# Second sets of seven products in three more up pairs of each layer, and the shared keys' row built later, in a two-layer hybrid decoder on one core

## The chip, the core and the metric

The kernel runs on one core of a Trainium2 chip. The metric is the device time of one execution, in microseconds (us). Names used below: PE is TensorE, PEld its weight loads, DVE is VectorE, ACT is ScalarE, POOL is GpSimd, SP is SyncE. A line such as L402 is that line of the kernel before. The change adds lines ahead of it, so the same code stands 5 lines lower in the changed kernel from there on (L402 is L407, L378 is L383, L596 is L601); L229 and L230 stay.

## The reference

Two layers over 256 tokens of width 2048: a chunked gated linear attention (GLA) in layer 0, a forgetting attention (FoX) in layer 1, each beside four heads of attention into 256 memory tokens. FoX's keys and values are projected from the residual after layer 0, once. Each layer ends in a gated feed-forward block with a causal convolution of width 3 between its projections:

```python
def conv_ffn(h, w_up, conv_w, conv_b, w_down):          # h: 256 x 2048
    u = causal_dwconv(h @ w_up, conv_w, conv_b)         # w_up: 2048 x 11264
    a, val = split_cols(u, [FFN_HIDDEN, FFN_HIDDEN])    # 5632 each
    return (jax.nn.silu(a) * val) @ w_down              # w_down: 5632 x 2048
def fox_shared_kv(x, g_kv, w_kv, b_f):
    hs = rmsnorm(x, g_kv)
    k, v, fl = split_cols(hs @ w_kv, [FOX_WIDTH, FOX_WIDTH, FOX_HEADS])
```

All of it is fp32. The outputs are one 256 x 2048 array.

## The kernel before, in words

**Products.** Every fp32 product is made of three matmuls of a rounded type. A weight tile of 128x1024, called raw, is loaded on SP's queue (L224); ACT rounds it to `whi` (L229) and DVE subtracts that from raw to get `wlo` (L230). The activations are kept in two such parts as well, so a product is (x high, w high), (x low, w high) and (x high, w low): two matmuls with `whi` and one with `wlo`. A tile pool holds 4 each of raw, whi and wlo, so ACT's split of a tile waits until PE has read the one four tiles earlier.

**Up pairs.** The up projection of a layer is done in 11 up pairs (0 to 10; up pair j//4 makes the gate and value columns of four hidden chunks j to j+3). An up pair runs over the 16 chunks k of the normed input; a chunk is one unit: one weight tile and 12 matmuls of 128x512 into four banks (two token blocks by two column halves). Matmuls of up and down pairs are issued in L402.

**Sets of seven products.** Two units with neighbouring chunks k and k+1 can be done together by a Strassen-like scheme with seven products instead of eight: 7x3 = 21 matmuls instead of 2x12 = 24. Such a set (`pair_steps`, L381 to L459) needs sums of the activations, prepared once for a chunk pair (`input_sums`, `token_sums`), and sums of the two weight tiles: raw2 tiles of their own, four subtractions of 128x512 on DVE (L427 to L430), and four splits by L377 on ACT and L378 on DVE (one of 512, three of 1024). After the last set of a pair, `early` scales what its products gave into tiles u; the pair's other units go on in the other banks, and `late` adds them up at the end.

Before, every up pair has one set, at k = 6. The first up pair after each of the first two parts of the hidden chunks (`PARTS`), which are up pairs 5 and 8, has a second at k = 11 through `more`, whose sums are computed anew each time into the tile `dsum` 0. The order of a pair's steps is that of k, so the sets stand at places 7 and 8, and 12 and 13. Down passes between the parts (f = 0 and 2, each 16 or 12 units) have sets too. The hidden chunks' pairs are ordered: up 0 to 4, two down passes, up 5 to 7, two down passes, up 8 to 10, then the last passes (the first of them called wide in the code).

**Work beside it.** An up pair's result is turned through DRAM on POOL's queue (`turn`, `far_away`, L640); when it is back, ACT makes the convolution's taps (L1384) and DVE adds and multiplies them (L1391, L1404). `tick` gives these steps out: after each unit the pair gains a credit (`drive`, 1.45 a unit), each step costs 0.5 to 1.0 of it, and a turn's first tap may come 8 ticks after the turn at the earliest.

**The shared keys' row.** FoX's key columns are three panels fk(0), fk(1), fk(2) (L333) of 8 units each, two units to a step for the first two (`two_tm`). The keys are scaled by 1/rms of each token, which must lie along a row: `row` (L585 to L599) builds two diagonal tiles dg on DVE (L594), multiplies them with ones on PE (L596, into the work bank ps_t) and copies the result on ACT (L598). It is called by a hook after unit 2 of fk(1); its first reader is L1160 (`keys`).

**Masks.** One constant tile `mask` of 1120 columns holds the identity, FoX's mask, the scan's mask, the level masks and an eye; it is loaded on SP's queue.

Of the kernel before, what the change touches and what calls it, by code (L numbers as in the profile page):

```python
# [36 lines left out]
SEVEN_MORE = 11  # L37

# [107 lines left out]
def _trunk(ctx: ExitStack, tc: tile.TileContext, xt, xtok, memt, wp, wgu, gns, gfin, cnv, par, msk, out):  # L146
# [13 lines left out]
    mask = const.tile([P, M_N], F32, name="mask")  # L160
# [3 lines left out]
    scanmask = mask[:, M_SCAN : M_SCAN + T]  # L164
# [216 lines left out]
    def pair_steps(units, src, sums, flip, pool, early, late):  # L381
# [360 lines left out]
    with tc.tile_pool(name="load", bufs=1) as lp:  # L742
# [57 lines left out]
        for u in range(8):  # L800
# [3 lines left out]
            elif u == 3:  # L804
                for b in range(2):
                    S.activation(mv[0][:, b, :], mv[0][:, b, :], AF.Copy, scale=nrm.col()[:, b : b + 1])
                with tc.issue_after(loads[-1].ins):
                    for i in range(KC):
                        nc.sync.dma_start(xf[i], xt[i])
                    nc.sync.dma_start(part, par)  # L810
                    nc.sync.dma_start(mask[:, M_FOX:], msk[:, M_FOX:])
# [20 lines left out]
    def gla(nx):  # L832
        h, mix = bufB, bufA
        with tc.tile_pool(name="gla", bufs=1) as gp:
            scratch[0] = gp

# [28 lines left out]
            def gates(hd):  # L865
# [7 lines left out]
                for c in range(2):  # L873
# [11 lines left out]
                    V.tensor_tensor_scan(bc[:, c, :], scanmask, mz, 0.0, ALU.mult, ALU.add)  # L885
# [110 lines left out]
            def core(hd):  # L996
# [36 lines left out]
                eye = mask[:, M_EYE:].bitcast(I32).unsqueeze(1).to_broadcast(ins.shape)  # L1033
                V.copy_predicated(ins, eye, ps[:, 192:320].rearrange("p (b t) -> p b t", b=2))
                for li, B in enumerate(LEVELS):
                    H = B // 4
                    p3 = levels[li].rearrange("p (b c) -> p b c", b=2)
                    m3 = mask[:, M_LVL + NVER * li : M_LVL + NVER * (li + 1)].bitcast(I32)
# [96 lines left out]
    def fox(nx, vt, stash):  # L1135
        hk, hq, mix = bufB, bufA, bufB
        with (
# [228 lines left out]
    def ffn(l, nx, h, m, ys, zs, landing, then, pool, temps, last=None, spare=None):  # L1366
        with tc.tile_pool(name=f"ffn{l}", bufs=1) as fp:
# [46 lines left out]
            def input_sums(k, tag="usum", at=None):  # L1414
# [4 lines left out]
                t = held(tag, k if at is None else at)  # L1419
# [76 lines left out]

            up_sums = {k: input_sums(k) for k in SEVEN_UP}
# [3 lines left out]
            more = {}  # L1501
            for p, (lo, hi) in enumerate(PARTS[:-1]):
                while done < hi + 4:
                    drive(up_pair(done, more))
                    more = {}
# [7 lines left out]
                more = {SEVEN_MORE: input_sums(SEVEN_MORE, "dsum", 0)}  # L1513
            lo, hi = PARTS[-1]
            while done < hi:
                drive(up_pair(done, more))
# [247 lines left out]
```

## Time and profile before

| | |
|---|---|
| time, median of 3 runs (lowest to highest) | 2221.74 us (2221.12 to 2222.1) |
| the profiled execution's own time | 2221.88 us |
| its span, first to last instruction | 2220.1 us |
| its mean granted TensorE clock | 0.999 |
| PE busy | 2207.2 us, 99% of the span |
| DVE busy | 1788.5 us, 81% |
| ACT busy | 1418.8 us, 64% |
| POOL busy | 136.1 us, 6% |
| up and down pairs of L402, layer 0 | 457.6 to 1110.8 us of the span |
| the same of layer 1 | 1500.8 to 2154.8 us |

The profile is one execution; the durations below come from it, and its own time is 0.14 us over the median. What lies between span and time is 1.78 us. A view by windows lists for a stretch of time the busy us of each engine with the count of its instructions (x); matmuls overlap in the records, so PE's own counts can include one that began earlier, while the count of PEld is the number of matmuls started. A group's row gives busy time and mean ns of one instruction, and behind a second bar the idle time of the engine just before them with what ended it. In the view in order of time a row has start, length, engine, line, operation and operands, and in brackets the idle time before it and its releaser.

### The profile page before, as it was taken

To read this page: it belongs to the slowest core of one execution; us is meant where nothing else is said; L and a number is where in the kernel's file an instruction comes from. 1 tells how busy PE (TensorE), PEld (TensorE's weight loads), DVE (VectorE), ACT (ScalarE), POOL (GpSimd) and SP (SyncE) were. 2 spreads that over 40 slices of the span, in tenths; PEclk is the share of its full clock that TensorE was granted. 3 is DMA by queue.
4 is the path that set the end of the run, shared out by engine and by line. 5 is a ranking of instruction groups with operands and counts; after the bars stand their busy time and mean duration, and the time that the engine had idled before them with its cause. 6 is when DMAs were issued, how large, how long until landed. Compare 5 with 4: busy or idle time off the path is not lost.

```text
span 2220.1 us, 30058 instructions
## 1 busy us (share of the span) xinstructions
PE 2207.2 (99%) x10323; PEld 1853.8 (84%) x10323; DVE 1788.5 (81%) x2654; ACT 1418.8 (64%) x2257; POOL 136.1 (6%) x257
## 2 busy tenths in 40 slices
PE   9999999999999999999999999999999999999998
PEld 7888888888888888888887998888888888888886
DVE  7768977688897888888978569668888888888896
ACT  6655664556787468656865455555787647665874
POOL 0000000001100000001110000000101000100100
PEclk9999999999999999999999999999999999999999
DMA  9767667778777567667777767777677757766674
GB/s 356 245 223 222 192 191 242 248 231 253 229 243 258 185 221 244 227 225 240 226 250 244 233 203 244 224 240 244 218 240 246 240 196 239 234 236 222 225 258 150
DMA packets 165633, 515.47 MB, mean 232 GB/s; under 512 B 20700, under 2 KB 41832, under 8 KB 165480
## 3 DMA queue, kind: packets, MB, share of 16 engines
q1 hardware_dynamic: 148488, 461.36, 63.6%
q0 software_dynamic: 16416, 51.40, 7.6%
q8 instruction: 81, 1.33, 0.2%
q10 hardware_dynamic: 576, 0.79, 0.1%
q14 instruction: 72, 0.59, 0.1%
HBM read 469.68 MB, written 43.79 MB: 231 GB/s over the span
## 4 chain that ended last, share of the span: by engine, by line
PE 95%; issue 2%; DVE 1%; DMA 1%; ACT 0%; POOL 0%; DVEq 0%; ACTq 0%; POOLq 0%
PE acc L402 30%; PE acc L333 23%; PE ps_s L402 15%; PE ps_o L402 7%; PE ps_t L402 7%; PE acc L305 3%; PE acc L260 3%; PE acc L363 2%; PE acc L258 1%; PE ps_s L333 1%; DVE wlo L230 0%; PE ps_s L1011 0%; DMA raw<-wp 0%; DMA fvt<-far 0%; PE ps_o L686 0%
## 5 line engine op out<-in xcount | busy, mean ns | idle before, releaser
L230 DVE TENSOR_TENSOR wlo<-raw,whi 128x1024 fp32r<-128x1024 f32 (+4 forms) x739 | 876.8, 1196 | 256.6 <-ACT whi L229 232.6
L229 ACT ACTIVATE whi<-raw 128x1024 fp32r<-128x1024 f32 (+4 forms) x739 | 760.4, 1037 | 447.4 <-PE acc L333 166.3
L333 PE MATMUL acc<-whi,B 128*128 128x512 f32 (+3 forms) x1248 | 292.0, 370 | 0.0
L377 ACT ACTIVATE whi<-raw 128x1024 fp32r<-128x1024 f32 (+1 forms) x136 | 129.8, 954 | 190.7 <-PE acc L402 75.5
L333 PEld LDWEIGHTS acc<-whi,B 128*128 128x128 f32 x1248 | 227.1, 188 | 28.0
L378 DVE TENSOR_TENSOR wlo<-raw,whi 128x1024 fp32r<-128x1024 f32 (+1 forms) x136 | 148.0, 1091 | 63.3 <-ACT whi L377 58.8
L402 PE MATMUL acc<-whi,mix 128*128 128x512 f32 x764 | 194.6, 389 | 0.0
L402 PE MATMUL acc<-whi,B 128*128 128x512 f32 x750 | 193.0, 389 | 0.0
L402 PEld LDWEIGHTS acc<-whi,mix 128*128 128x128 f32 x764 | 143.3, 188 | 30.2 <-ACT whi L229 0.2
L402 PEld LDWEIGHTS acc<-whi,B 128*128 128x128 f32 x750 | 140.8, 188 | 29.6
L333 PE MATMUL acc<-wlo,B 128*128 128x512 f32 (+3 forms) x624 | 158.6, 369 | 0.0
L333 PEld LDWEIGHTS acc<-wlo,B 128*128 128x128 f32 x624 | 114.6, 188 | 14.5
L1384 ACT ACTIVATE tap<-yzu,cw 128x256 f32<-128x256 f32 x264 | 123.5, 531 | 1.5 <-DMA yzu<-far 1.5
L1384 ACT ACTIVATE tap<-fvt,cw 128x256 f32<-128x256 f32 x264 | 123.3, 529 | 0.8 <-DMA fvt<-far 0.8
L1391 DVE TENSOR_TENSOR tap<-tap,tap 128x1024 f32<-128x1024 f32 x88 | 107.3, 1219 | 1.1 <-ACT tap L1384 1.0
L402 PE MATMUL acc<-wlo,mix 128*128 128x512 f32 x382 | 107.5, 389 | 0.0
L402 PE MATMUL acc<-wlo,B 128*128 128x512 f32 x375 | 107.3, 389 | 0.0
L402 PE MATMUL ps_s<-whi,mix 128*128 128x512 f32 x386 | 106.1, 389 | 0.0
L402 PE MATMUL ps_s<-whi,B 128*128 128x512 f32 x342 | 93.5, 389 | 0.0
L402 PEld LDWEIGHTS ps_s<-whi,mix 128*128 128x128 f32 x386 | 72.5, 188 | 15.3
L402 PEld LDWEIGHTS acc<-wlo,mix 128*128 128x128 f32 x382 | 71.7, 188 | 15.0
L402 PEld LDWEIGHTS acc<-wlo,B 128*128 128x128 f32 x375 | 70.4, 188 | 14.7
(498 smaller groups left out, 3802.3 us busy)
## 6 DMA issues: line engine op xcount, KB each, us to landing
raw<-wp SPq DMA_DIRECT2D x743, 512.0 KB, 4.5
fvt<-far POOLq DMA_DIRECT2D x100, 128.0 KB, 5.3
raw<-wp SPq DMA_DIRECT2D x32, 384.0 KB, 3.5
far<-yu POOLq DMA_DIRECT2D x22, 512.0 KB, 5.8
far<-yzu POOLq DMA_DIRECT2D x22, 512.0 KB, 5.4
yzu<-far POOLq DMA_DIRECT2D x88, 128.0 KB, 5.0
raw<-wp SPq DMA_DIRECT2D x24, 388.0 KB, 4.7
x<-xtok SPq DMA_DIRECT2D x8, 512.0 KB, 6.6
```

The costliest lines, as they stand in the source:

```text
L229: casts.append(S.activation(hi[:, s], raw[:, s], AF.Copy))
L230: lows.append(V.tensor_tensor(lo[:, s], raw[:, s], hi[:, s].bitcast(F32), ALU.subtract))
L258: mm = TE.matmul(acc[p][c][:, :T], w[:, s], both[:, 0, :], start=False, stop=end and j == 3)
L260: mm = TE.matmul(acc[p][c], w[:, s], both, start=u == j == 0, stop=end and j == 3)
L305: mm = TE.matmul(acc[b][:, :n], src[kcs[j] - base][:, part, b * P : (b + 1) * P], w, start=u == 0 and low == part == j == 0, stop=u == end ...
L333: mm = TE.matmul(acc[b][:, :n], src[kc - base][:, part, b * P : (b + 1) * P], ready[low][:, j * n : (j + 1) * n], start=i == low == part = ...
L363: mm = TE.matmul(acc[b][:, :n], src[kc - base][:, part, b * P : (b + 1) * P], w, start=i == low == part == j == 0, stop=i == end and low = ...
L377: casts.append(S.activation(hi[:, :n], src, AF.Copy))
L378: lows.append(V.tensor_tensor(lo[:, :n], src, hi[:, :n].bitcast(F32), ALU.subtract))
L402: r = TE.matmul(bank[name], x, w, start=name not in begun, stop=last)
L1384: S.activation(by_run(taps[i][:, s, c, i:]), zs[slot][:, :, 2 * c + s], AF.Copy if i else AF.Identity, bias=0.0 if i else w[3], scale=w[2 ...
L1391: V.tensor_tensor(taps[0], taps[0], taps[n][:, :, :, :T], ALU.add)
```

## The change

Up pairs 1, 5, 6, 8 and 9 (`MORE_IN`) have a second set, at chunks 11 and 12, instead of 5 and 8. In these pairs both sets come two places earlier than by their chunk (`ahead` = 2): at the 5th and the 10th place, with the single units in their own order around them. The sums of chunks 11 and 12 are computed once a layer, within up pair 0 after its unit 13, into a tile of their own that stays. The turns' waits and the credit are altered: 7 ticks instead of 8 for the first turn of a pair that stands ahead of a pair of `MORE_IN`, and 1.7 instead of 1.45 a unit within such a pair. To have room, `mask` keeps 512 columns; the other 608 come in a tile `gmask` of the GLA stage, loaded on POOL's queue. The hook that built the shared keys' row after unit 2 of fk(1) goes; `row` is called after unit 3 of fk(2).

```diff
+MORE_IN = (1, 5, 6, 8, 9)
...
-    mask = const.tile([P, M_N], F32, name="mask")
+    mask = const.tile([P, M_SCAN], F32, name="mask")
...
-    def pair_steps(units, src, sums, flip, pool, early, late):
+    def pair_steps(units, src, sums, flip, pool, early, late, ahead=0):
...
+        single = [k for k in range(n) if k not in sums and k - 1 not in sums]
         plan = []
-        k = 0
-        while k < n:
-            plan.append(k)
-            k += 2 if k in sums else 1
+        at = 0
+        while at < n:
+            if at + ahead in sums:
+                plan.append(at + ahead)
+                at += 2
+            else:
+                plan.append(single.pop(0))
+                at += 1
...
+            gmask = gp.tile([P, M_N - M_SCAN], F32, name="gmask")
+            nc.gpsimd.dma_start(gmask, msk[:, M_SCAN:])
...
-            two_tm([fk(0), fk(1)], 8, 2, {(1, 2): nx.row,
-                                          (1, 3): lambda: nx.land(spare[1]), (1, 5): nx.take})
+            two_tm([fk(0), fk(1)], 8, 2, {(1, 3): lambda: nx.land(spare[1]), (1, 5): nx.take})
             step = fk(2)
             for u in range(8):
                 step(u)
+                if u == 3:
+                    nx.row()
...
-            def up_pair(j, more={}):
+            def up_pair(j):
...
-                turns = [turn(j + 2 * h_, 8) for h_ in range(2)]
+                second = j // 4 in MORE_IN
+                turns = [turn(j + 2 * h_, 7 if not h_ and j // 4 + 1 in MORE_IN else 8) for h_ in range(2)]
...
-                return pair_steps(where["up", l, j], h, {**up_sums, **more}, count[2] % 2, pool, early, late)
+                return pair_steps(where["up", l, j], h, {k: up_sums[k] for k in (*SEVEN_UP, SEVEN_MORE)[: 1 + second]},
+                                  count[2] % 2, pool, early, late, 2 * second)
...
+                if k == 13:
+                    up_sums[SEVEN_MORE] = input_sums(SEVEN_MORE)
...
+            def drive_up(j):
+                drive(up_pair(j), 1.7 if j // 4 in MORE_IN else 1.45)
...
-                more = {SEVEN_MORE: input_sums(SEVEN_MORE, "dsum", 0)}
```

**Place one: PE in up pair 1 of layer 0, behind its fourth unit.** The names B_99 to B_114 are chunks 0 to 15 of the normed input, ps_o, ps_s, ps_t and acc are banks, usum is a tile of sums. Before, the fifth unit follows, chunk 4 (B_103):

```order
L402 MATMUL ps_o<-whi,B_103 128x512 x2
L402 MATMUL ps_s<-whi,B_103 128x512 x4
L402 MATMUL ps_t<-whi,B_103 128x512 x2
L402 MATMUL ps_o<-wlo,B_103 128x512
L402 MATMUL ps_s<-wlo,B_103 128x512 x2
L402 MATMUL ps_t<-wlo,B_103 128x512
L402 MATMUL ps_o<-whi,B_104 128x512 x2
```

In the changed kernel the set of chunks 6 and 7 (B_105, B_106) stands there, and chunk 4 begins behind its first matmuls:

```order
L407 MATMUL acc<-whi,B_105 128x512 x2
L407 MATMUL acc<-wlo,B_105 128x512
L407 MATMUL ps_o<-whi,B_106 128x512 x2
L407 MATMUL ps_s<-whi,usum 128x512
L407 MATMUL ps_o<-wlo,B_106 128x512
L407 MATMUL ps_s<-whi,usum 128x512
L407 MATMUL ps_s<-wlo,usum 128x512
L407 MATMUL acc<-whi,usum 128x512 x6
L407 MATMUL ps_s<-whi,B_106 128x512 x2
L407 MATMUL acc<-wlo,usum 128x512 x2
L407 MATMUL ps_o<-whi,B_103 128x512 x2
```

The set moved up by two places; a second such set, of chunks 11 and 12, follows after chunks 4, 5 and 8, where there were 24 matmuls of single units.

**Place two: PE in the shared keys' panels.** B_111 and B_112 are two chunks of a weight tile of fk(1); dg and onesr are the operands of the row's two products. Before, these lie amid the matmuls with `whi` of one unit:

```order
L333 MATMUL acc<-whi,B_111 128x512 x2
L333 MATMUL acc<-whi,B_112 128x512 x2
L333 MATMUL acc<-whi,B_111 128x512 x2
L596 MATMUL ps_t<-dg,onesr 128x256
L333 MATMUL acc<-whi,B_112 128x512
L596 MATMUL ps_t<-dg,onesr 128x256
L333 MATMUL acc<-whi,B_112 128x512
L333 MATMUL acc<-wlo,B_111 128x512
```

In the changed kernel they stand between the fourth and the fifth unit of fk(2):

```order
L333 MATMUL acc<-wlo,B_105 128x512
L333 MATMUL acc<-wlo,B_106 128x512
L333 MATMUL acc<-wlo,B_105 128x512
L333 MATMUL acc<-wlo,B_106 128x512
L601 MATMUL ps_t<-dg,onesr 128x256 x2
L333 MATMUL acc<-whi,B_107 128x512 x2
L333 MATMUL acc<-whi,B_108 128x512 x2
L333 MATMUL acc<-whi,B_107 128x512 x2
```

Only the two products and ACT's copy of them move; DVE builds the diagonals dg at the same place of its order as before. Over the whole program PE has 18 matmuls of 128x512 fewer.

More of the change, by code (lines that the diff above doesn't have):

```diff
@@ L810, in _trunk @@
                     nc.sync.dma_start(part, par)
[L811 removed]
+                    nc.sync.dma_start(mask[:, M_FOX:], msk[:, M_FOX:M_SCAN])
         with tc.issue_after(nrm.made.ins):
@@ L1500, in ffn @@
             done = 4
-            more = {}
             for p, (lo, hi) in enumerate(PARTS[:-1]):
                 while done < hi + 4:
-                    drive(up_pair(done, more))
-                    more = {}
+                    drive_up(done)
                     done += 4
@@ L1512, in ffn @@
                 sums.clear()
-                more = {SEVEN_MORE: input_sums(SEVEN_MORE, "dsum", 0)}
             lo, hi = PARTS[-1]
             while done < hi:
-                drive(up_pair(done, more))
-                more = {}
+                drive_up(done)
                 done += 4
```

12 lines of the change are left out of this document (6 added, 6 removed).

## The prediction

> **What bounds the kernel now.** I read the page first: its line of busy times, then the chain of work that ended last.
>
> ```profile
> PE 2207.2 (99%) x10323; PEld 1853.8 (84%) x10323; DVE 1788.5 (81%) x2654; ACT 1418.8 (64%) x2257; POOL 136.1 (6%) x257
> ...
> PE 95%; issue 2%; DVE 1%; DMA 1%; ACT 0%; POOL 0%; DVEq 0%; ACTq 0%; POOLq 0%
> PE acc L402 30%; PE acc L333 23%; PE ps_s L402 15%; PE ps_o L402 7%; PE ps_t L402 7%; PE acc L305 3%; PE acc L260 3%; PE acc L363 2%; PE acc L258 1%; PE ps_s L333 1%; DVE wlo L230 0%; PE ps_s L1011 0%; DMA raw<-wp 0%; DMA fvt<-far 0%; PE ps_o L686 0%
> ```
>
> PE is busy for 99% of the span and makes 95% of the chain; L402, which the change touches, is 59% of it. DVE's 81% is an average, so I next read it stage by stage: a window for each pair, cut at the first matmul of the pair and of the next one. In order: up pair 1, up pair 4, down passes f = 0 (without a set) and f = 2 (two sets), up pairs 5 (two sets), 6, 8 (two sets), 9, 10, and the wide pass, all of layer 0.
>
> ```profile
> core 0: us, PE busy (x) PEld busy (x) DVE busy (x) ACT busy (x) POOL busy (x), PEclk, DMA share, GB/s
> 500.58:543.54 42.96, 42.96 (x191) 35.47 (x189) 34.11 (x40) 32.03 (x51) 5.46 (x10) 1.00 0.78 240
> 629.45:672.41 42.96, 42.96 (x190) 35.48 (x189) 39.19 (x51) 33.02 (x54) 5.47 (x10) 1.00 0.78 247
> 672.41:715.94 43.53, 43.53 (x193) 36.04 (x192) 33.71 (x37) 29.74 (x49) 5.46 (x10) 1.00 0.80 271
> 715.94:758.34 42.40, 42.40 (x187) 34.92 (x186) 38.81 (x52) 22.30 (x26) 0.00 (x0) 1.00 0.54 180
> 758.34:800.75 42.41, 42.41 (x187) 34.92 (x186) 33.71 (x38) 22.93 (x25) 0.00 (x0) 1.00 0.57 191
> 800.75:843.72 42.97, 42.97 (x190) 35.48 (x189) 35.19 (x44) 32.60 (x52) 5.50 (x10) 1.00 0.79 247
> 951.41:993.81 42.40, 42.40 (x187) 34.91 (x186) 36.52 (x46) 23.46 (x26) 0.00 (x0) 1.00 0.60 195
> 993.81:1036.78 42.97, 42.97 (x190) 35.48 (x189) 34.16 (x40) 32.08 (x51) 5.51 (x10) 1.00 0.78 248
> 1036.78:1079.77 42.99, 42.99 (x190) 35.48 (x189) 38.44 (x50) 33.26 (x54) 5.46 (x10) 1.00 0.73 234
> 1079.80:1112.80 33.00, 33.00 (x147) 27.20 (x146) 32.09 (x40) 21.70 (x34) 5.48 (x10) 1.00 0.74 235
> ```
>
> Two things are to be seen. PE fills each window wholly, at a clock of 1.00, so the length of a pair is its matmuls: 192 (PEld's count) without a set, 189 with one, 186 with two. And DVE has room, but not the same everywhere: 3.8 us idle in up pair 4, 8.9 in pair 1, 0.9 in the wide pass (97% busy).
>
> **The change: six more sets.** A set takes 3 matmuls away. The windows give the price at once, with all that a set costs PE in slower matmuls: one set takes a pair from 43.53 to 42.97 us, a second from 42.97 to 42.40, so **0.56 us a set**, read off as up pair 1 or 6 against up pair 5 or 8. (That is less than three matmuls of 43.53/192 = 0.227 us, 0.68 us together: the matmuls of a set come slower. A pair with two sets has 12 single units of 12 matmuls and 42 in its sets, so these take (42.40 − 144×0.2267)/42 = 0.232 us each.) Up pairs 1, 6 and 9 of two layers get one more: 6 × 0.56 = **3.4 us**.
>
> The Trainium skill, in "TensorE: Matmul & The Clock Gate", section "Back-to-back issue gap", gives an isolated matmul of 512 columns N/2.4 + 2.5, about 216 ns, and a sustained stream of them about 131 ns. By 216 ns six sets would save 3.9 us, by 131 ns 2.4 us. The trace agrees with neither: its pitch is 227 ns, and the saving is taken from the windows.
>
> What hides the other side of a set? On DVE it adds three splits of 1024, one of 512 and four subtractions, and takes two splits of L230 away; on ACT likewise.
>
> ```profile
> L230 DVE TENSOR_TENSOR wlo<-raw,whi 128x1024 fp32r<-128x1024 f32 x673 | 814.1, 1220 | 211.3 <-ACT whi L229 193.1 <-PE acc L333 4.2 <-issue 4.1
> L229 ACT ACTIVATE whi<-raw 128x1024 fp32r<-128x1024 f32 x673 | 704.9, 1056 | 391.2 <-PE acc L333 116.2 <-PE acc L402 87.5 <-PE ps_t L402 74.0
> L378 DVE TENSOR_TENSOR wlo<-raw,whi 128x1024 fp32r<-128x1024 f32 x102 | 124.9, 1225 | 51.2 <-ACT whi L377 49.5
> L377 ACT ACTIVATE whi<-raw 128x1024 fp32r<-128x1024 f32 x102 | 108.3, 1062 | 147.6 <-PE ps_t L402 60.2 <-PE acc L402 60.1 <-DVE raw L428 9.7
> L427 DVE TENSOR_TENSOR raw<-raw 128x512 f32<-128x512 f32 x34 | 23.5, 690 | 0.6
> L378 DVE TENSOR_TENSOR wlo<-raw,whi 128x512 fp32r<-128x512 f32 x34 | 23.4, 689 | 12.2 <-ACT whi L377 9.3 <-PE ps_t L402 2.7
> L377 ACT ACTIVATE whi<-raw 128x512 fp32r<-128x512 f32 x34 | 21.5, 633 | 43.1 <-PE acc L402 15.5 <-PE ps_t L402 13.2 <-DVE wlo L230 9.7
> ```
>
> DVE: 3×1.225 + 0.689 + 4×0.690 − 2×1.220 = **4.7 us**. ACT: 3×1.062 + 0.633 − 2×1.056 = 1.7 us. So up pair 1 would have 34.1 + 4.7 = 38.8 us of DVE in 42.4 (91%), pair 6 39.9 (94%), pair 9 38.9 (92%). The f = 2 window is a row of this kind today: two sets, DVE 38.81 of 42.40, PE without a pause. That is why I take the stall at nothing. ACT, at most 34.3 of 42.4, is far from its end. The splits come first in DVE's order, so what does not fit is pushed on: pair 10 (38.44 now) may rise to some 41 of 43, before the wide pass with 0.9 us of room; there the cover is thin, and a microsecond not hidden is a microsecond of PE. Bounds per set: −0.56 us of PE if all is hidden, and +4.7 − 0.56 if none of it is. I take the first, since the nearest row is at 92%.
>
> The sets' places (5th and 10th) hold the splits apart by three single units, as in pairs 5 and 8 before, and leave five units, not three, between the last set and the pair's end; `early` has 2 × 12 × 0.227 = 5.4 us more time. Their sums cost DVE once a layer in up pair 0 rather than twice behind the down passes: a little less in all, nothing to PE, and their tile is free long before it is read, in up pair 1. Their weights come on SP's queue in the order of the sets; a set loads the same bytes as two units.
>
> **The row.** The row's two products wait for DVE today, and PE waits with them, since its queue is in order. PE first, then DVE, in order of time:
>
> ```profile
> 1199.94 1.52 PE L333 MATMUL acc<-whi,B 128*128 128x512 f32 x6
> 1203.46 0.38 PE L596 MATMUL ps_t<-dg,onesr 128*128 128x256 f32 x1 [2.00 <-DVE dg L594]
> 1203.68 0.40 PE L333 MATMUL acc<-whi,B 128*128 128x512 f32 x1
> ```
>
> ```profile
> 1200.36 1.23 DVE L230 TENSOR_TENSOR wlo<-raw,whi 128x1024 fp32r<-128x1024 f32 x1
> ...
> 1201.57 1.23 DVE L230 TENSOR_TENSOR wlo<-raw,whi 128x1024 fp32r<-128x1024 f32 x1
> 1202.70 0.18 DVE L589 CAST y<-ny 128x2 fp32r<-128x2 f32 x1
> 1202.91 0.16 DVE L590 TENSOR_TENSOR y<-ny,y 128x2 fp32r<-128x2 f32 x1
> 1202.99 0.75 DVE L594 TENSOR_TENSOR dg<-mask,y 128x256 fp32r<-128x256 f32 x2
> 1203.66 3.51 DVE L230 TENSOR_TENSOR wlo<-raw,whi 128x1024 fp32r<-128x1024 f32 x3
> ```
>
> Six matmuls from 1199.94 at 0.227 us end their issue at 1201.30, and the product starts at 1203.46: 2.16 us lost (the view's 2.00 counts from the records' end). Moved behind fk(2)'s fourth unit, the products come 90 matmuls later in PE's order, at 1201.3 + 20.4 = 1221.7, with dg made by about 1203.7 since DVE's order there is the same. What is late next? Without the pause PE finishes the two remaining `whi` matmuls at 1201.30 + 0.45 = 1201.76 and needs this unit's `wlo`, ready about 1201.6 by DVE's row at 1200.36 (1.23 long): 0.17 us to spare. The following unit's is needed eight matmuls later, at 1203.57, and ready at 1202.80 (the row at 1201.57). Bounds: 0 (the whole wait comes back at the next split) to 2.16 us; I take **2.1**, since DVE's split is done before PE can ask for it, and a few units on ACT waits for PE again, the first row below:
>
> ```profile
> 1207.68 1.06 ACT L229 ACTIVATE whi<-raw 128x1024 fp32r<-128x1024 f32 x1 [1.77 <-PE acc L333]
> ...
> 1204.29 0.39 ACT L598 ACTIVATE row<-ps_t 128x256 f32<-128x256 f32 x1 [1.49 <-PE ps_t L596]
> ...
> 1228.12 1.42 DVE L1160 TENSOR_TENSOR fkt<-fky,row 128x256 f32<-128x256 f32 x4
> ```
>
> At the new place the row must be there for its first reader, the last row, which would be at about 1228.1 − 2.2 = 1226. The products at 1221.7 and ACT's copy of 0.4 us behind a split of 1.06 leave some 3 us.
>
> **The rest.** The masks' second part leaves SP's queue for POOL's at the start. POOL issues it where it has a memset today, and its first reader is the scan:
>
> ```profile
> 82.71 0.31 POOL L493 MEMSET narrow<- 128x256 f32 x1 [81.73 <-DMA raw<-wp]
> 137.13 0.69 DVE L885 TENSOR_TENSOR_SCAN bc<-mask,gm 128x256 f32<-128x256 f32 x1
> ```
>
> 54 us between them hide a transfer of 0.3 MB; if that cover were gone the scan would be late by what the transfer lacks. The identity and FoX's mask come earlier, if anything. Cost: nothing. The taps' new due times only re-time them: the credit of a changed pair is 12 × 1.7 = 20.4 against 14 × 1.45 = 20.3, and two turns cost 2 × 10.2 by the steps' own costs. Some first taps wait a little for their return today, and one tick less can lengthen that on ACT:
>
> ```profile
> 901.45 1.71 ACT L1384 ACTIVATE tap<-fvt,cw 128x256 f32<-128x256 f32 x4 [0.77 <-DMA fvt<-far]
> 1945.66 3.31 ACT L1384 ACTIVATE tap<-yzu,cw 128x256 f32<-128x256 f32 x8 [1.48 <-DMA yzu<-far]
> ```
>
> Neither made PE wait. ACT's next splits stand behind such a tap, and a tick is a unit, 12 × 0.227 = 2.7 us, so the worst is a wait of 1.48 + 2.7 = 4.2 us. Tiles split ahead cover it: with four of each and one in use, up to three units, 8.2 us. I take nothing.
>
> **Sum.** 3.4 + 2.1 = 5.5 us off the profiled execution's 2221.88: 2216.4. The median is 0.14 lower: **2216.2 us**.
>
> **The rivals.** *Late lows (A).* DVE stays under 100% by windows but is late inside them, in pairs 6 to 7 and 9 to 10 and in the wide pass, where sets, taps and what was pushed on meet. For: 94% in pair 6, 97% in wide. Against: 92% in f = 2 without a pause. Price: pair 9's 4.7 us fall on pair 10 (4.5 us idle) and wide (0.9 us); if half of it shows, 2.4 us a layer, 4.7 in all: about 2221, and with a smaller part 2218 to 2219.
>
> *DVE is the bound (B), the other side.* The splits of the second set wait for DVE, its queue keeps the order, and the taps behind them fall due at the same time. A set that stalls PE by more than 5.5/6 = 0.92 us makes the kernel slower; with none of the 4.7 us hidden it is 2216.4 + 28 = 2244, with half 2230. For: the idle DVE of layer 0 in pairs 8 to 10 together is 5.9 + 8.8 + 4.6 = 19.2 us, and the added work is within it, so against.
>
> *The row's wait stays (C).* The 0.17 us is too little, or the products wait elsewhere: only the sets count, 2218.4.
>
> *Returns late (D).* The Trainium skill's "SBUF — State Buffer", section "SBUF: two separate sides", says that DMAs from POOL's queue can starve while certain DVE operations hold a port that both share. With more DVE work, POOL's issues would then be later.
>
> ```profile
> L640 POOL DMA_DIRECT2D fvt<-far x100 | 54.6, 553 | 114.9 <-issue 37.7 <-ACT whi L377 35.4 <-DMA far<-yu 15.3
> ```
>
> The row shows 553 ns an issue while DVE is busy 81% of the span, so I see no such wait here. Late returns by one unit in each of ten pairs would cost up to ten times 0.77 to 1.48 us on ACT, and on PE at most a part: 2217 to 2222.
>
> **How the numbers follow.** About 0.2%, 4.4 us, is what a measurement of this kernel can tell from no change. Forecast (2215.2 to 2217.3): 0.60. A: 0.15, C: 0.09, D: 0.05, all mostly within 0.2%; B: 0.11. Faster takes the forecast and a little of A and D: 0.62. Same: 0.26. Slower: B with the tail of A, 0.12. The range reaches from 2215.0 (row and sets in full with half a microsecond beside them) over A, C and D to 2222.0.
>
> **What would show it.** Right: windows of 42.4 us for up pairs 1, 6 and 9 in both layers; no wait of a product for dg; DVE near 39 to 40 us in those windows and 41 in pair 10, with PE still full. Wrong: pauses of PE that end with a low split (L378, L230), above all in pairs 7, 10 and wide; DVE over 42 us in a pair; a wait of the fk panels' matmuls for `wlo`; a scan that waits for gmask; taps waiting for returns by more than 2 us.

## The result and the profile after

| | before | after |
|---|---|---|
| median of 22 runs each | 2222.32 us | 2225.76 us |
| lowest to highest | 2221.12 to 2225.54 | 2223.38 to 2229.57 |
| ratio, with its 95% interval | | 1.0013 (1.0007 to 1.0019) |
| profiled execution: time, span | 2221.88, 2220.1 | 2224.02, 2221.1 |

The forecast was 2216.2 us. The kernel became 3.4 us slower by the medians. The profiled execution of after has the shortest span of its 22 runs (2221.1 to 2227.8 us), so it shows the least of what went wrong; a second profile of the same kernel is among the experiments.

The lines' numbers in after are not all 5 higher: the splits of a set stay at L377 and L378, its subtractions L427 to L430 are L432 to L435, the taps' L1384, L1391 and L1404 are L1393, L1400 and L1413 (one more where an experiment moves the copies), and L1160 is L1168. The copies of `early` for up pairs are L1472 and L1473 in before, L1482 and L1483 in after.

The page of after first, its busy times and its chain:

```profile
PE 2207.3 (99%) x10305; PEld 1848.4 (83%) x10305; DVE 1805.8 (81%) x2676; ACT 1426.0 (64%) x2267; POOL 136.4 (6%) x258
...
PE 92%; issue 3%; DMA 2%; ACT 1%; DVE 1%; POOL 1%; SPq 0%; ACTq 0%; DVEq 0%; POOLq 0%
```

The 18 matmuls are gone (10323 to 10305), and PE's share of the chain fell from 95% to 92%. The windows, cut as in the prediction, show where: in order up pairs 1, 2, 3, 6, 7, 10 and the wide pass of layer 0.

```profile
500.31:543.00 42.69, 42.69 (x188) 34.70 (x186) 36.32 (x43) 30.34 (x47) 5.48 (x10) 1.00 0.70 220
543.00:586.40 43.40, 43.28 (x191) 35.33 (x189) 38.65 (x48) 35.73 (x60) 5.46 (x10) 1.00 0.79 251
586.40:629.80 43.40, 43.28 (x191) 35.33 (x189) 39.18 (x50) 33.55 (x55) 5.47 (x10) 1.00 0.73 240
801.12:843.54 42.42, 42.42 (x188) 34.93 (x186) 36.37 (x43) 30.62 (x47) 5.46 (x10) 1.00 0.71 210
843.54:887.16 43.62, 43.28 (x190) 35.33 (x189) 39.02 (x51) 35.49 (x59) 5.46 (x10) 1.00 0.77 249
1036.72:1080.12 43.40, 43.28 (x190) 35.34 (x189) 39.34 (x51) 35.70 (x61) 5.47 (x10) 1.00 0.74 244
1080.12:1113.60 33.48, 33.25 (x146) 27.16 (x145) 32.53 (x41) 22.22 (x33) 5.47 (x10) 1.00 0.75 235
```

Pairs 6 and 9 are 42.42 us, 0.55 under before, as forecast; pair 1 is 42.69 here and 42.42 in a second profile. But the one-set pairs that follow a two-set pair (2 and 3 behind 1, 7, 10), whose 189 matmuls did not change, are longer: pairs 2, 3 and 10 by 0.41 to 0.45, pair 7 by 0.67, wide by about 0.48. Layer 1 does the same. DVE is 38.7 to 39.3 us of the 43.4 to 43.6 in the pairs that pause, 89 to 91%, no larger a share than in pair 4 of before (39.19 of 42.96), which had no pause.

What pauses is one instruction in each. In order of time, up pair 3, PE and then ACT and DVE of after:

```profile
603.17 0.61 PE L407 MATMUL ps_o<-whi,B 128*128 128x512 f32 x2
603.62 0.40 PE L407 MATMUL ps_s<-whi,usum 128*128 128x512 f32 x1
603.86 0.39 PE L407 MATMUL acc<-wlo,B 128*128 128x512 f32 x1
...
605.71 0.63 PE L407 MATMUL acc<-wlo,usum 128*128 128x512 f32 x2
606.46 0.73 PE L407 MATMUL acc<-whi,usum 128*128 128x512 f32 x2
```

```profile
604.29 0.60 ACT L1482 ACTIVATE fvt<-acc 128x512 f32<-128x512 f32 x1 [0.76 <-PE acc L407]
604.78 0.68 ACT L1483 ACTIVATE fvt<-acc,ny 128x512 f32<-128x512 f32 x1
605.35 1.06 ACT L377 ACTIVATE whi<-raw 128x1024 fp32r<-128x1024 f32 x1
```

```profile
603.54 0.68 DVE L435 TENSOR_TENSOR raw<-raw 128x512 f32<-128x512 f32 x1
604.14 1.22 DVE L378 TENSOR_TENSOR wlo<-raw,whi 128x1024 fp32r<-128x1024 f32 x1
```

The same place in before, two rows of PE (the last matmul of the first product and the first one that needs the fourth weight), then ACT:

```profile
603.30 0.39 PE L402 MATMUL acc<-wlo,B 128*128 128x512 f32 x1
...
606.31 0.63 PE L402 MATMUL acc<-whi,usum 128*128 128x512 f32 x2
```

```profile
603.73 0.60 ACT L1472 ACTIVATE fvt<-acc 128x512 f32<-128x512 f32 x1 [0.77 <-PE acc L402]
604.22 0.68 ACT L1473 ACTIVATE fvt<-acc,ny 128x512 f32<-128x512 f32 x1
604.79 1.06 ACT L377 ACTIVATE whi<-raw 128x1024 fp32r<-128x1024 f32 x1
```

`early` copies the set's first product out of its bank twice, and in this pair these copies stand in ACT's order ahead of the set's fourth split. They wait for PE's last matmul of that product. Before, that was at 603.30 and the split ended at 605.85, ahead of PE's need at 606.31. Now that matmul stands at 603.86, behind three others that it preceded, the split ends at 606.41, PE would start at 606.17 (two matmuls of 0.23 after 605.71) and starts at 606.46; the next matmul follows 0.34 us behind, not 0.23, so 0.40 of the window's 0.45 us are found. PE waits for itself: first product, two copies, split, fourth weight. DVE was in time: its fourth subtraction (L435), which that split reads, ended at 604.22, over a microsecond ahead of the split. Nothing in the diff moves these instructions within such a pair; their order is made when the program is built, and it came out otherwise in pairs 2 and 10 (where before the split stood ahead of the copies) and 3 and 7. In all eight such pairs of both layers the split stands behind the copies, DVE's fourth subtraction was done 0.4 to 1.4 us ahead of what PE needed, and in the two wide passes one copy stands so too.

The row did what was forecast. PE runs through where it lost 2.16 us (about 1201), and the products stand free at their new place:

```profile
1222.94 0.40 PE L601 MATMUL ps_t<-dg,onesr 128*128 128x256 f32 x2
1223.42 0.39 ACT L603 ACTIVATE row<-ps_t 128x256 f32<-128x256 f32 x1
1227.06 1.42 DVE L1168 TENSOR_TENSOR fkt<-fky,row 128x256 f32<-128x256 f32 x4
```

Its first reader has 3.25 us to spare, as worked out. One more pause is in layer 1's up pair 0 (43.76 us, 42.94 before), taken up below.

### The profile page after: what moved, and what is told of

It is laid out like the page before. It is cut to its first block, busy times and chain, and to the rows that moved or that the text cites. A ratio compares the mean times of both kernels' runs of the same rounds, so it can differ in the third digit from the quotient of the medians.

```text
span 2221.1 us, 30080 instructions
## 1 busy us (share of the span) xinstructions
PE 2207.3 (99%) x10305; PEld 1848.4 (83%) x10305; DVE 1805.8 (81%) x2676; ACT 1426.0 (64%) x2267; POOL 136.4 (6%) x258
## 4 chain that ended last, share of the span: by engine, by line
PE 92%; issue 3%; DMA 2%; ACT 1%; DVE 1%; POOL 1%; SPq 0%; ACTq 0%; DVEq 0%; POOLq 0%
PE acc L407 28%; PE acc L333 23%; PE ps_s L407 14%; PE ps_o L407 7%; PE ps_t L407 7%; PE acc L305 3%; PE acc L260 3%; PE acc L363 2%; PE ps_s L333 2%; PE acc L258 1%; DMA fvt<-far 1%; ACT whi L377 1%; POOL fvt L645 1%; PE ps_s L1018 0%; DMA far<-tblk 0%
## 5 line engine op out<-in xcount | busy, mean ns | idle before, releaser
L230 DVE TENSOR_TENSOR wlo<-raw,whi 128x1024 fp32r<-128x1024 f32 (+4 forms) x727 | 861.0, 1193 | 272.4 <-ACT whi L229 245.2
L229 ACT ACTIVATE whi<-raw 128x1024 fp32r<-128x1024 f32 (+4 forms) x727 | 744.6, 1037 | 422.4 <-PE acc L333 161.1
L377 ACT ACTIVATE whi<-raw 128x1024 fp32r<-128x1024 f32 (+1 forms) x160 | 152.1, 953 | 201.5 <-PE acc L407 56.2
L378 DVE TENSOR_TENSOR wlo<-raw,whi 128x1024 fp32r<-128x1024 f32 (+1 forms) x160 | 173.3, 1085 | 61.2 <-ACT whi L377 57.7
L1393 ACT ACTIVATE tap<-yzu,cw 128x256 f32<-128x256 f32 x264 | 122.6, 530 | 0.0
L1393 ACT ACTIVATE tap<-fvt,cw 128x256 f32<-128x256 f32 x264 | 122.5, 529 | 0.0
L1400 DVE TENSOR_TENSOR tap<-tap,tap 128x1024 f32<-128x1024 f32 x88 | 107.1, 1217 | 1.4 <-ACT tap L1393 1.2
```

The lines of the kernel that those rows point to most:

```text
L229: casts.append(S.activation(hi[:, s], raw[:, s], AF.Copy))
L230: lows.append(V.tensor_tensor(lo[:, s], raw[:, s], hi[:, s].bitcast(F32), ALU.subtract))
L377: casts.append(S.activation(hi[:, :n], src, AF.Copy))
L378: lows.append(V.tensor_tensor(lo[:, :n], src, hi[:, :n].bitcast(F32), ALU.subtract))
L1393: S.activation(by_run(taps[i][:, s, c, i:]), zs[slot][:, :, 2 * c + s], AF.Copy if i else AF.Identity, bias=0.0 if i else w[3], scale=w[2 ...
L1400: V.tensor_tensor(taps[0], taps[0], taps[n][:, :, :, :T], ALU.add)
```

## The experiments

Names: **O**, the order on ACT, as just read. **L**, rival A of the prediction, DVE is late. **C**, a load of PE's code falls amid a transfer (not the prediction's rival of that letter). **N**, transfers that land late. Each result stands beside runs of the kernel before on the same chip, whose median was 2222.2 to 2223.3.

**Copies behind the split, in after and in before.** In both `early` functions:

```diff
+                    with tc.issue_after(casts[-1].ins):
-                    S.activation(u[0, 1], bank["p1"], AF.Copy)
-                    S.activation(u[0, 0], bank["p1"], AF.Copy, scale=scale(0))
+                        S.activation(u[0, 1], bank["p1"], AF.Copy)
+                        S.activation(u[0, 0], bank["p1"], AF.Copy, scale=scale(0))
```

> The changed kernel, with the copies of the first product (in early, of up and down pairs) queued on ACT behind the set's fourth split. Theory O (the order on ACT): in up pairs 2, 3, 7, 10 and the wide pass of both layers the profile after shows PE waiting at the fourth weight tile, 0.40 to 0.68 us longer windows, since ACT makes two copies of 1.07 us together ahead of that split; here these pauses go, windows fall back to 42.95 to 43.0 us, and the time falls by about 4.5 us (the sum of the ten longer windows, 0.41+0.45+0.68+0.41+0.47+0.40+0.43+0.67+0.40+0.81 = 5.1, less what DMA landings make of the last), to about 2221, 1 to 2 us under the kernel before. Theory L (DVE is late): the fourth tile's low split is late too, the pauses stay within 0.1 us, time unchanged at about 2225.7.

> The kernel before with the same edit of the copies. Theory O: the copies stand ahead of the fourth split in up pairs 3, 4 and 7 there too, but with 0.4 us to spare, so no pause is taken away: same time within 0.5 us of 2222.3. Theory L says the same. If it is faster by over 1 us, the copies cost something that the profile of before does not show.

Measured: 2223.49 us (0.9999 of before, 0.9990 to 1.0007), so 2.3 us under after; and 2223.24 (1.0002, 0.9993 to 1.0010), no change in before. That is half of the 4.5 us that I gave O. The windows of up pairs 2, 3 and 7 of layer 0 and 2 and 7 of layer 1 (its pair 3 is 43.38 us) say where:

```profile
542.68:585.64 42.96, 42.96 (x191) 35.47 (x189) 38.45 (x47) 33.86 (x56) 5.49 (x10) 1.00 0.79 255
585.64:628.99 43.35, 43.25 (x190) 35.33 (x189) 38.87 (x48) 33.19 (x55) 5.49 (x10) 1.00 0.76 243
842.78:886.49 43.71, 43.23 (x190) 35.39 (x189) 39.42 (x50) 34.79 (x58) 5.50 (x10) 1.00 0.76 241
1586.45:1629.45 43.00, 43.00 (x190) 35.47 (x189) 38.05 (x47) 32.80 (x54) 5.49 (x10) 1.00 0.79 248
1886.52:1929.53 43.01, 43.01 (x190) 35.47 (x189) 38.73 (x50) 34.09 (x56) 5.49 (x10) 1.00 0.76 248
```

Pair 2 is free, and pair 10 too (42.96 and 43.00 us); pair 3 keeps its pause, and so does pair 7 of layer 0. In pair 3 ACT now waits for DVE's fourth subtraction (L435), which stands behind tap work (L1414) and the split of the third tile (L378) in DVE's order:

```profile
604.57 1.06 ACT L377 ACTIVATE whi<-raw 128x1024 fp32r<-128x1024 f32 x1 [1.36 <-DVE raw L435]
```

```profile
601.33 0.69 DVE L1414 TENSOR_TENSOR cv<-tap 128x512 f32<-128x512 f32 x1
601.93 0.69 DVE L434 TENSOR_TENSOR raw<-raw,raw 128x512 f32<-128x512 f32 x1
602.63 1.23 DVE L378 TENSOR_TENSOR wlo<-raw,whi 128x1024 fp32r<-128x1024 f32 x1
603.77 0.68 DVE L435 TENSOR_TENSOR raw<-raw 128x512 f32<-128x512 f32 x1
```

That wait is a new one. In after the subtraction stood ahead of the third tile's split and ended 17.8 us into the pair (604.22 − 586.40); here it ends at 18.8 (604.45 − 585.64), and the fourth split has to begin at 18.7 if PE is not to wait (605.35 less 0.29 in after). So the edit moved more than the copies: the build gave DVE another order too, and the pause that stays in pair 3 isn't the one of after. By after's own rows the copies account for its pauses in the eight one-set pairs, whose windows together are 3.85 us longer than with the sets undone (below). With the copies moved they are 1.63 us longer: 2.2 us gained, as in the medians, and what is left is L. No run moves the copies and nothing else.

**The parts apart.** After with `MORE_IN = (5, 8)`, all else as changed; and before with only the row moved.

> The changed kernel with MORE_IN = (5, 8): the sets are as many as before (18 matmuls more), at the 5th and 10th place in these two pairs; the row, the masks, the sums and the taps' times stay changed. Theory O: ACT's order in the one-set pairs is that of before, so no new pause there, and the row's 2.1 us show: about 2220.2. If the row's wait comes back elsewhere (rival C) or the other parts cost, about 2222.3 or more.

> The kernel before with only the row moved behind fk(2)'s fourth unit. Both theories of the sets say nothing of it. If the wait of 2.16 us is won as forecast: about 2220.2. The profile after has 1.1 us of new pauses between the wide pass of layer 0 and up pair 0 of layer 1 and 0.8 in that pair's set; if these come from the moved row (loads that do not start earlier with it) the gain is about 0.3, 2222.

Measured: 2221.13 us (0.9990, 0.9981 to 0.9999) and 2220.9 (0.9989, 0.9980 to 0.9998). The row alone is worth 2.0 us against its own runs of before (by the interval 0.4 to 4.4), and places, masks, sums, credits and taps beside it cost nothing that shows (0.2 us). In its profile the wait of 2.16 us is gone, but layer 1's up pairs begin only 1.26 us earlier (1499.58 for 1500.84), since PE waits 1.4 us for weight splits at the entry to layer 1 (1177 to 1183, ahead of the row), 0.4 in before. These waits differ from profile to profile without the row as well: 1.1 us with the copies moved in before. So the six sets made 2221.13 into 2225.76: 4.6 us more, where 3.4 less were forecast. It is those 8.0 us that have to be found. By its median the row alone is the fastest kernel of the study that computes all of the reference, though not clear of the two next to it (2221.13, and 2221.64 below).

**The same kernel again.**

> The changed kernel once more, for a second profile. The first had a span of 2221.1 us, while its runs have spans up to 2225. Theory O+L (ACT's copies ahead of the fourth split, and DVE late with the fourth subtraction): the pauses in up pairs 2, 3, 7, 10 and wide come back at the same places within 0.1 us; what differs from profile to profile is up pair 0 of layer 1, whose set waits for a transfer, and the wide pass of layer 1, where DVE is solid. Theory N (transfers that land late): pauses at other places, of other lengths.

Measured: 2227.58 us in its one run, span 2225.8. Pairs 2, 3, 7 and 10 of both layers repeat to 0.02 us (43.40, 43.40, 43.63, 43.40): they are fixed in the program. What differs is elsewhere: up pair 0 of layer 1 is 44.93 us instead of 43.76, the last units of layer 1's wide pass wait 1.3 us for a product of the taps, and up pair 0 of layer 1 begins 1.6 us later.

**Less work for DVE.** The copies behind the split, and the two sums of the taps (L1400) left out: the convolution's second and third tap are computed and not added.

```diff
-                        steps += [(1.0, lambda: add_tap(1)), (1.0, lambda: add_tap(2)), (0.5, silu),
+                        steps += [(1.0, int), (1.0, int), (0.5, silu),
```

> The changed kernel with the copies behind the fourth split, and with the two sums of the taps (2 x 1.22 us of DVE for each of two turns of an up pair, 4.9 us a pair) left out: the convolution's second and third tap are made and not added. Theory L: the pauses that stayed with the copies moved (up pairs 3 and 7: 0.4 to 0.8 us, wide of layer 1: 2.3) are DVE's backlog; with 4.9 us less they go, all up pairs are 42.4 or 43.0 us, and the time is about 2221.1 - 3.3 = 2217.8 (six sets under the kernel with its sets undone). Theory O alone or N: the pauses stay, about 2223.5.

Measured: 2217.6 us (0.9979, 0.9970 to 0.9988). Up pairs 3 and 7 of layer 0 (layer 1's are 42.95 and 42.97 us):

```profile
585.69:628.65 42.96, 42.96 (x190) 35.48 (x189) 34.13 (x42) 33.17 (x54) 5.47 (x10) 1.00 0.77 244
842.41:885.39 42.98, 42.98 (x190) 35.48 (x189) 35.02 (x44) 33.60 (x55) 5.47 (x10) 1.00 0.79 256
```

With 4.9 us less DVE a pair every pause behind the sets is gone, and so are those of the wide passes and of the entry to layer 1; only that of layer 1's up pair 0 stays. L is shown for the pauses that the kernel with the copies moved had left, not for those of after. The time is 3.5 us under the sets undone (2221.13), as six sets should bring, but in part by luck: in the windows the six two-set pairs give 3.1 us, pair 0 of layer 1 loses 1.6, and 2.2 come from the entry to layer 1, whose waits are not the sets' own. So the 5.9 us (2223.49 to 2217.6) say little of how much L is worth.

**The sets at their old places, and the taps' old times.** One without the 2 in `2 * second`, one with 8 ticks and 1.45 everywhere.

> The changed kernel with the sets at the places of their chunks (7th and 12th), not two places earlier. If the earlier places make the backlog (five units after the last set, the splits of the next pair's set then fall amid the taps), the pauses of up pairs 2, 3, 7, 10 go and the time is 2217.8 to 2221. If it is the added DVE work wherever the set stands, the pauses move to the two-set pairs or stay: 2225 or more, slower than the changed kernel by up to 3 us, since three units, not five, lie behind the last set.

> The changed kernel with the taps' due times and credit of before (8 ticks and 1.45 everywhere). The prediction put these at nothing: 2225.8 then. If 1.45 spreads the taps' work into the next pair (12 x 1.45 = 17.4 of the 20.4 that two turns cost), the one-set pairs after a two-set pair get about 3 credits of taps more, 3 us of DVE, and longer pauses there: 2228 to 2232.

Measured: 2243.43 us (1.0095, 1.0082 to 1.0109, four runs) and 2227.32 (1.0023, 1.0014 to 1.0032). The first is the largest effect of the study: without the earlier places the sets would have cost 17.7 us more, and my 3 us were far off. Up pairs 1 and 2 of layer 0, and ACT in pair 2:

```profile
500.30:544.21 43.91, 43.13 (x187) 34.60 (x186) 34.96 (x41) 28.82 (x43) 5.45 (x10) 1.00 0.68 210
544.21:589.20 44.99, 43.25 (x190) 35.33 (x189) 40.57 (x50) 37.41 (x64) 5.47 (x10) 1.00 0.78 250
```

```profile
562.33 0.60 ACT L1482 ACTIVATE fvt<-ps_o 128x512 f32<-128x512 f32 x1 [3.43 <-PE ps_o L407]
562.83 0.68 ACT L1483 ACTIVATE fvt<-ps_o,ny 128x512 f32<-128x512 f32 x1
563.40 2.01 ACT L377 ACTIVATE whi<-raw 128x1024 fp32r<-128x1024 f32 x2
```

The two-set pair itself pauses now, and the next one by 2.0 us. More of the work is pushed into it (40.57 us of DVE, 38.65 in after), but the 2.0 us are O again, and more of it: the copies, which wait for PE's first product, stand ahead of the third split too, whose data DVE had ready at 561.75. Pairs 2, 7 and 10 of both layers have this pause. In the two-set pairs ACT's third and fourth splits mostly wait for DVE's subtractions, which is L. Of the 17.7 us, the windows put 10.0 on the one-set pairs and 7.7 on the two-set pairs; what the old places would cost with the copies moved was not run.

The old tap times are 1.6 us over after, but the two intervals overlap: unclear, and less than the 2 to 6 us that I expected if they spread. In its profile the one-set pairs are 6.3 us longer than with the sets undone, in after 3.85, and partly in other places: pair 7 of layer 0 is 44.94 us, pair 2 of layer 1 44.81, pair 3 is free.

**Sums on POOL.** The copies behind the split, and L1400 on POOL.

```diff
-                    V.tensor_tensor(taps[0], taps[0], taps[n][:, :, :, :T], ALU.add)
+                nc.gpsimd.tensor_tensor(taps[0], taps[0], taps[n][:, :, :, :T], ALU.add)
```

> The changed kernel with the copies behind the fourth split and the taps' two sums on POOL, not on DVE: DVE loses 4.9 us a pair, POOL (6% busy) takes them, and its queue also issues the turns' transfers. Theory L: as with these sums left out, 2217.6, if POOL needs no more than 3 us a sum and disturbs nothing. If POOL and DVE hold each other up at a shared port (the Trainium skill, SBUF, State Buffer, section on two separate sides), DVE's splits get longer than 1.22 us while a sum runs, the pauses stay or grow: 2224 or more.

Measured: 2244.17 us (1.0090, 1.0075 to 1.0106, five runs). The groups, then one stretch in order of time:

```profile
L1400 POOL TENSOR_TENSOR tap<-tap,tap 128x1024 f32<-128x1024 f32 x88 | 216.7, 2463 | 463.5 <-ACT tap L1394 371.5 <-DVE temp L1494 34.9 <-DVE fvt L1494 34.6
L230 DVE TENSOR_TENSOR wlo<-raw,whi 128x1024 fp32r<-128x1024 f32 x661 | 894.8, 1365 | 264.0 <-ACT whi L229 250.0 <-issue 3.1 <-PE acc L258 2.7
```

```profile
587.23 5.07 POOL L1400 TENSOR_TENSOR tap<-tap,tap 128x1024 f32<-128x1024 f32 x2 [9.69 <-ACT tap L1394]
590.37 3.00 DVE L230 TENSOR_TENSOR wlo<-raw,whi 128x1024 fp32r<-128x1024 f32 x1
```

A sum takes 2.46 us on POOL, twice DVE's 1.22, and a split that meets one takes 3.00 instead of 1.22. Over 661 splits that is 661 × (1.365 − 1.217) = 98 us, 1.1 us for each of the 88 sums, nearly what DVE was spared; DVE's busy time as a whole is 1809.1 us, 1806.7 with the copies moved alone. The one split shown ends 1.07 us after POOL's second sum. That is what the Trainium skill says in "SBUF — State Buffer", section "SBUF: two separate sides": the pair of ports that both share is an exclusive lock, also for a DVE operation with two inputs from SBUF against a GpSimd operation that reads it. The trace agrees, and the prices are above.

**The load of code.** In after, the weights of the set in layer 1's up pair 0 (L426, two tiles) are issued on SP's queue when the write of a turned block ahead of them has landed. SP's queue, before and then after:

```profile
1504.11 0.49 SPq L635 DMA_DIRECT2D far<-blk  x1
1508.97 0.80 SPq L421 DMA_DIRECT2D raw<-wp  x2
```

```profile
1503.02 0.33 SPq L640 DMA_DIRECT2D far<-blk  x1
1508.81 0.81 SPq L426 DMA_DIRECT2D raw<-wp  x2
```

From issue to issue 4.9 us before, 5.8 in after, 6.9 in its second profile. The transfers of that one, from the issue of a weight load just ahead of the write at 1504.0 to the landing (a view of 1504 to 1511.5 us with the rate in 40 slices):

```profile
GB/s 44 0 0 0 0 218 22 218 87 131 306 175 131 218 371 175 306 350 371 415 371 393 415 371 240 153 66 0 22 0 0 22 22 22 22 44 22 0 0 0
...
q8 instruction: 1, 0.02, 0.8%
```

The bulk is through after 27 slices, and a trickle of 22 GB/s, one packet of 4 KB in a slice, holds up the end. Amid the window lies one packet of an instruction queue, q8, whose 80 packets in all are about PE's 20,600 matmuls and weight loads in blocks of 256; so I take it for a load of PE's code. In seven profiles it falls amid the write (after, its second profile, the kernels with five second sets but for the two below), and the write takes 5.8 to 6.9 us; in before, in the copies in before, the sets undone and the row alone it falls ahead of the write's issue, 4.2 to 4.9 us. With 18 matmuls instead of 9 to warm up, PE's stream of instructions is as long at that point as in before.

> The changed kernel with 18 instead of 9 warming matmuls at the start, so that PE's stream of instructions before layer 1 is as long as in the kernel before. Theory C (a load of PE's code amid a write): in the kernels with five second sets a load of instructions falls 2.5 to 3.5 us after the issue of the last turned block's write, that write takes 5.8 to 6.9 us instead of 4.2 to 4.9, and the weights of up pair 0's set in layer 1, whose tile waits for it, come late; with nine matmuls more ahead it falls before the issue as in the kernel before, the write takes under 5 us, and that up pair 43.0 us instead of 43.8 to 44.9. The start costs 0 to 3.8 us (9 matmuls of 0.43). Rival: the write is longer for another reason, the pair stays at 43.8 or more.

Measured: 2224.91 us (1.0008, 0.9999 to 1.0017). SP's queue and the pair's window:

```profile
1505.52 0.33 SPq L640 DMA_DIRECT2D far<-blk  x1
1510.51 0.80 SPq L426 DMA_DIRECT2D raw<-wp  x2
```

```profile
1502.26:1545.28 43.02, 43.02 (x190) 35.32 (x189) 36.67 (x71) 26.23 (x40) 0.00 (x0) 1.00 0.70 230
```

The packet now comes ahead of the issue, the write takes 5.0 us and the pair 43.02: C holds for this pause, which was 0.8 to 2.0 us. The net gain is 0.9 us, by intervals that overlap with after's (to 1.0017 here, from 1.0007 there); the start is 1.5 us longer by layer 0's first up pair. One profile seems to speak against C. With three pairs (below) the packet, at 1500.80, came ahead of the write's issue, and the write still took 5.7 us:

```profile
1500.75 0.33 SPq L224 DMA_DIRECT2D raw<-wp  x1
1501.37 0.75 SPq L640 DMA_DIRECT2D far<-blk  x1
```

But it came only 0.57 us ahead, 0.05 us behind the issue of the weight load in front of the write; in the six profiles with a write of 4.2 to 5.0 us it came 0.2 us or more ahead of that load's issue too. So all 14 profiles agree if it is that load's issue that counts. No run tests this alone, and how the packet holds up the write is open.

**Fewer sets, and both cures.** `MORE_IN = (1, 5, 8)` with the copies behind; and the full change with copies behind and 18 warming matmuls.

> MORE_IN = (1, 5, 8) with the copies behind the fourth split: of the three new second sets only that of up pair 1. Two more sets in all save 1.1 us against 2221.1 (the sets undone). Theory L: up pair 1 has the most room (8.9 us of DVE idle), but its push falls on pair 3, which kept a pause of 0.4 us in each layer with the copies moved; pairs 7, 10 and wide are free. 2220.8 and one load of code less well placed at most, 2222.5.

> The changed kernel with the copies behind the fourth split and 18 warming matmuls. If the two causes add (copies 2.3 us, code load in the write 0.9 us after the longer start), about 2225.8 - 3.2 = 2222.6, which is the kernel before within 0.5 us. Theory L: up pairs 3 and 7 and the wide pass keep their pauses (0.4, 0.7 and up to 2.3 us), since DVE's fourth subtraction is late there; up pair 0 of layer 1 is 43.0 us. Under 2221.1 (the sets undone) would say that DVE's backlog was not the rest; over 2224, that one of the two gains was chance.

Measured: 2221.64 us (0.9993, 0.9984 to 1.0002) and 2222.75 (0.9998, 0.9989 to 1.0007). In the first, pairs 7, 10 and wide are free and pair 3 pauses by 0.4, as expected; its two sets gain nothing over having none, for in the windows they give 1.0 us, and pair 3 of both layers takes 0.9 and pair 0 of layer 1, behind the late write, 1.0. In the second both cures show in the windows: the write takes 4.9 us and pair 0 of layer 1 43.12, and the rest stays: pair 3 is 43.35 and 43.37 us. The time is only 0.7 us under that with the copies moved alone, by intervals that are nearly the same, so it does not show that the gains add. It has a wait that none of the other kernels with the taps' sums on DVE shows, in the first down pass after pair 7, where PE stands for 1.9 us behind ACT's splits and these behind a tap whose turn came back late:

```profile
908.36 1.71 ACT L1394 ACTIVATE tap<-fvt,cw 128x256 f32<-128x256 f32 x4 [6.00 <-DMA fvt<-far]
```

**The 8.0 us by windows.** Lengths against the profile with the sets undone, in us:

| | after | its second profile | copies moved | copies moved, no tap sums |
|---|---|---|---|---|
| the six pairs with a new set (1, 6, 9) | −3.01 | −3.28 | −2.92 | −3.08 |
| the eight one-set pairs behind them (2, 3, 7, 10) | 3.85 | 3.82 | 1.63 | 0.02 |
| up pair 0 of layer 1 | 0.81 | 1.98 | 1.95 | 1.59 |
| wide pass of layer 0 to the start of that pair | −0.35 | 1.40 | 0.09 | −2.24 |
| wide pass of layer 1 to the end | 1.08 | 3.00 | 2.42 | 0.01 |
| span (with the start and the other pairs) | 2.21 | 6.87 | 2.78 | −4.01 |

The sets bring 2.9 to 3.3 us where 3.4 were forecast. The second row is O in after, and DVE with the copies moved; the third is the late write. The two stretches below it differ most between the two profiles of one kernel.

## Why the prediction was wrong

- **Sets, 0.56 us each: right.** 42.40 to 42.42 us in five of the six pairs, and in all six in the second profile: 3.3 us in its windows.
- **Row, 2.1 us: right** as far as it can be told. 2.0 us alone, with 0.4 to 4.4 by the interval; only 0.17 us were to spare at the next low split, and in one profile, with the sets undone, 0.3 us came back there.
- **Masks, sums, places, tap times at nothing: right** as far as 0.2 us, for the kernel with its sets undone. That the earlier places save the new sets 17.7 us, I didn't see: I counted 5.4 us more for `early` and gave it no price.
- **"That is why I take the stall at nothing": wrong, and this is the step that failed.** I judged a set's cover by DVE's share of a window and by one row, the f = 2 pass at 92%. The pauses came at 89 to 91%, and not in the two-set pairs but in the one-set pairs behind them: 3.85 us in eight pairs, and about half a microsecond in each wide pass. What a set needs is not room in the window but that its fourth tile be ready, through first product, copies and split on ACT, and through four subtractions on DVE, each in an order that the build decides. Pair 3 of before had 606.31 − 605.85 = 0.46 us to spare there. I had treated those pairs as untouched, and worked out DVE's pushed work (41 us in pair 10, 39.3 measured) as if only a full window could hurt. More was pushed than I said: the two-set pairs 1, 6 and 9 have 36.3 us of DVE, not 38.8 to 39.9, and pairs 2 and 7 behind them 38.7 and 39.0 instead of 37.3. Nor does a set's work come first in DVE's order, as I wrote of the splits: tap work stands ahead of the third and the fourth subtraction (L1414, L434 and L435 in the rows of pair 3 above). In pairs 2, 7 and 10 the fourth subtraction ends 1.0 to 1.8 us later in the pair than before; that this is why the build put the copies first is likely, but no run shows it.
- **Rival A** named the price (2221, 4.7 us lost) and three places (7, 10, wide), but put it on DVE's lows. In after the pauses end with ACT's fourth split, behind the copies, and pairs 2 and 3 have them too; DVE is what holds up the kernels with the copies moved. What was lost is 8.0 us by the medians, not 4.7, so with the row's gain the sum came out over before.
- **Rivals B, C and D.** B's mechanism as I wrote it (a saturated engine in the new pairs) did not come: pairs 6 and 9 don't pause. C, the row's wait, fell but for the 0.3 us. D's sentence on POOL's issues: they stay at 552 to 556 ns (L645), even with POOL and DVE blocking each other. Returns that ACT waits 3 us or more for show up in five profiles of the experiments, none of them of the changed kernel itself. 4.0 us (with the nine warming matmuls) did not reach PE, as I had said of 4.2; 6.0 did, by 1.9.
- **Open:** the 8.0 us as a sum. The pauses in the one-set pairs and wide passes make some 4.8 of them and the late write 0.8 to 2.0. The rest, at the entry to layer 1 and from its wide pass to the end, differs by 1.8 and 1.9 us between two profiles of the same kernel, and is not taken apart.

## What to carry to other kernels

A stage in which the bounding engine never waits tells nothing of how nearly it does: before adding work beside it, take the spare time of the tightest operand, instruction by instruction, also in the neighbours of the place that is changed. When an order is made by a scheduler, compare it in those neighbours too, for an instruction that waits for the bounding engine and stands ahead of one that feeds it. A share of 90% is safe or not by how the work lies, so a gain of 0.2% that leans on it needs its own experiment. And an edit that moves one instruction can move others with it when a scheduler makes the order: compare the other engines' rows before the rest that stays is put down to the next cause.

## What the runs showed of the hardware

One packet of 0.02 MB of an instruction queue, by its count a load of PE's own code, went with a write of 512 KB that took 5.7 to 6.9 us instead of 4.2 to 5.0 when it came behind the issue of the load ahead of that write, and PE waited for what stood behind the write; nine matmuls fewer ahead of it, three sets of layer 0, were enough to move it there, and nine more to move it away. And a sum on POOL holds up DVE's two-input splits (1365 ns instead of 1217 on the average), for 1.1 us a sum.
